# Fewer background taps ahead of attention, more folded products at the boundaries, and two lasting sets of padded key tiles in a two-layer diffusion backbone

## The chip, the cores and the metric

The kernel runs on one core of a Trainium2 chip. The metric is the device time of one execution in microseconds; lower is better. The time of the kernel before is the median of 3 runs, and a profile of one more execution is read below.

## The reference

A hybrid backbone with `D_MODEL = 1024` and two layers is computed for two groups of tokens with the same weights: a prompt of 128 tokens (its attention reads only the prompt) and a sample of 256 tokens (its attention also reads 128 cached keys). A layer has three sublayers, a feed-forward network, a mixer and a second feed-forward network, and each ends with a residual and a layer norm:

```python
h = modulate(0)
x = layer_norm(ALPHA * x + 0.5 * mod[:, 2] * swiglu(h, w_ffn_in[l, 0], w_ffn_out[l, 0]), ...)
h = modulate(1)
mix, k, v = token_mixer(h, l, p, ctx_k, ctx_v)
x = layer_norm(ALPHA * x + mod[:, 5] * mix, ...)
h = modulate(2)
x = layer_norm(ALPHA * x + 0.5 * mod[:, 8] * swiglu(h, w_ffn_in[l, 1], w_ffn_out[l, 1]), ...)
```

`token_mixer` projects its input once and cuts the result into queries, keys, values, the conv branch, the pool branch and three gates:

```python
z = h @ w_in[l] + b_in[l]                       # q, k, v, cg, pu, gt
o = rms_norm(diff_attention(q, kk, vv, lam))    # softmax of map 1 minus lam * softmax of map 2, 4 heads
att_out = o @ w_att_o[l]
u = depthwise_conv(a * sigmoid(g), conv_dw_w)   # 31 taps
conv_out = silu(layer_norm(u)) @ w_conv_o[l]
pool_out = multiscale_pool(pu) @ w_pool_o[l]
merged = ga * att_out + gc * conv_out + gp * pool_out
return merged @ w_out[l] + b_out[l], k, v
```

## The kernel before

**Tiling.** Features lie on the 128 partitions and all 384 tokens on the free axis. Each product is made from a high and a low part of weight and activation, so it is three matmuls (`mm3`, L409, L410 and L411; L732, L733 and L735 at a boundary). Weights come in 388 units of up to 128x1024; a unit is 24 matmuls of TensorE. `wh`, the high part, is a cast by ScalarE (L345), and `wl` a subtraction by VectorE (L353).

**Order.** The program is written out as one sequence, and each engine runs its part in that order. `begin(key)` (L374) opens a unit: it advances a step counter, casts the weights of the unit four ahead, runs the closures that are due at this step (`at(n, fn)` puts one n steps ahead; those due together run in the order in which they were put), then takes the low part of the weights, and then pops `bg_rate` closures from the background queue `bg` (a fraction is carried over). Only then are the unit's own matmuls written. So a matmul in a due closure stands ahead of the unit's 24, and what it waits for holds up all of them.

**The mixer** (L1057). `BG = (qk, v, pu, attention and gates, start)` gives the rate of the background queue in each stage: eight q/k units (two of them in one group), four v units (`w_v`), two pool units (`w_in` 16 and 17), then 24 gate units during which attention runs. The queue holds, in this order, 62 taps of the conv branch (one VectorE instruction each, L1118 from the third on), `conv_chain`, and 14 steps of the pool branch and its `chain`. `conv_chain` puts the stages of the conv branch's norm at `CONV_AT = (2, 4, 5, 6, 8, 9, 10, 11)` steps after it is popped: `c1` (the sum's matmuls, L1137), `c2` (broadcast of the mean, L541), `c2b`, `c3` (the squares' matmuls, L548), `c4` twice (broadcast of the scale L541, then `cz` and `cth` on ScalarE), `c5` (`ch`, L1186 on ScalarE) and `c6` (`cl`, L1192 on VectorE). The first `cp` unit, `cp0`, multiplies `ch` and `cl`; right after its `begin` a loop runs steps ahead of time until both exist.

**Attention** is ten tasks: `prompt_task` twice, then `sample_task` eight times (four heads, two blocks of queries), one task every two steps. Each has four closures at `ATT_AT` steps: `a` (scores, L1478 for the prompt, L1428 and L1429 for the sample; maxima L1483 or L1434 on VectorE; exponentials `e` on ScalarE), `b_` (L1499 or L1446 on VectorE), `c` (transposes of `e`, L1505 or L1451), `d` (product with the values L1460, whose result ScalarE reads twice, into `o`, L1463, and into `jk`, L1465). `stack(h)` makes the padded tiles of a head: `Q`, `K`, `QL` and `KL`; half of each `KL` tile is zero, written by GpSimd (L1401).

**Banks.** Six PSUM banks ("mm") serve the units and the scores. Two ("sm", from `sbank()`) serve all the rest in turn: `L1460`, `L1451`, the transposes, and the stages `c1` to `c4`. The third claim on "sm" has to wait until the first has been read.

**A boundary** (`ln_end`, L708). The norm's sum is folded into the next sublayer: the first group of four weight tiles multiplies `fold[k]`, k = 0 to 7, before mean and scale are known. `main(k0, k1)` writes 12 matmuls for each k (four tiles, three each). The order on TensorE is `main(0, 2)`, the statistics (L548, tile `tot`), `main(2, 3)`, the two broadcasts (L541), `main(3, 6)`, then the tail with k = 6 and 7. The statistics need the last tile's sums (L745 and L746 on VectorE); the broadcasts need the chain of small VectorE instructions in `ln_scale` (up to L704). There are five such boundaries with a next sublayer; i is the place in its layer of the sublayer that ends, and i = 1 is the mixer.

Of the kernel before, what the change touches and what calls it, by code (L numbers as in the profile page):

```python
# [11 lines left out]
F32 = mybir.dt.float32  # L12
F32R = mybir.dt.float32r
# [81 lines left out]

BG = (3, 3, 3, 2.5, 2)
CONV_AT = (2, 4, 5, 6, 8, 9, 10, 11)
ATT_AT = (0, 1, 2, 4)  # L100
GATE_AT = 32
# [137 lines left out]
class Kernel:  # L239
# [468 lines left out]
    def ln_end(self, b7, ab, keys):  # L708

        nc, st = self.nc, self.lns  # L710
        s = st["s"]
        l, i = divmod(s, 3)
        y7 = self.X[:, 7, :]
        sq = self.slot(name="sq")
        mm = nc.tensor.matmul
        outs = None
        if keys:
            self.fold_cols(7)
            ws = self.group(keys)
            self.held = 4  # L720
            outs = [self.bank() for _ in keys]
        for lo, hi, c in SEGS:
            nc.vector.scalar_tensor_tensor(y7[:, lo:hi], b7[:, lo:hi], st["g"][:, 0, 7, c:c + 1], y7[:, lo:hi],
                                           ALU.mult, ALU.add)
            nc.scalar.activation(sq[:, lo:hi], y7[:, lo:hi], AF.Square)

        def main(k0, k1):
            for k in range(k0, k1):
                yh, yl = self.fold[k]
                sl = slice(128 * k, 128 * k + 128)  # L730
                for (wh, wl), o in zip(ws, outs):
                    mm(o[:, :NX], wh[:, sl], yh, start=k == 0, stop=False)  # L732
                    mm(o[:, :NX], wl[:, sl], yh, start=False, stop=False)  # L733
                for (wh, wl), o in zip(ws, outs):
                    mm(o[:, :NX], wh[:, sl], yl, start=False, stop=False)  # L735

        if keys:
            ma = 2
            main(0, ma)
            self.after.append(lambda: self.fold_tile(7))  # L740
            for _ in range(8):
                self.run_after()
        merge = keys
        if merge:
            nc.vector.tensor_add(st["s1"], st["s1"], y7)  # L745
            nc.vector.tensor_add(st["s2"], st["s2"], sq)  # L746
        else:
            st["late"]()
        if keys:
            self.prep(self.cur + 1)  # L750
            if self.n_prep == self.cur + 1:
                self.prep_h()
        if merge:
            tot = self.ln_stat(st["s1"], st["s2"])
        else:
            b = self.ln_stat(y7, sq)
            tot = self.tiny(6)
            nc.vector.tensor_add(tot, st["pre"], b[:, :6])
        rm = self.ln_scale(tot)
        if keys:  # L760
            if self.half:
                self.prep_l()
            for _ in range(3):
                self.run_after()
            main(ma, 3)
        R, M = self.sbank(), self.sbank()
        self.bcast(R, rm[:, 0:3])
        self.bcast(M, rm[:, 3:6])
        if keys:
            Rs = self.slot(name="R")  # L770
            nc.scalar.copy(Rs, R[:, :NT])
            self.RM = Rs, M
            main(3, 6)

            def tail():
                for (wh, wl), o in zip(ws, outs):
                    for k in (6, 7):
                        c = 128 * k
                        self.mm3(o[:, :NX], wh[:, c:c + 128], wl[:, c:c + 128], *self.fold[k], False, k == 7)
                del ws[:]  # L780
                self.fold = [None] * 8
                self.lead = 2
        ts = [None] * 9
        xs = [None] * 8

        def mul(m):
            if m < 8:
                ts[m] = self.slot(name="t")
                nc.vector.tensor_mul(ts[m], self.X[:, m, :], R[:, :NT])

        def add(m):
            if m < 8:
                nc.vector.tensor_add(ts[m], ts[m], M[:, :NT])  # L793

        def upd(m):
            nc.scalar.activation(self.X[:, m, :], ts[m], AF.Identity, bias=self.lnbs[:, l, i, m:m + 1],
                                 scale=self.par(("lng", l, i), 1, m))

        if not keys:
            Ms = self.slot(name="M")  # L800
            nc.scalar.copy(Ms, M[:, :NT])
            mul(0)
            for m in range(8):
                mul(m + 1)
                if m % 2 == 0:
                    nc.gpsimd.tensor_add(ts[m], ts[m], Ms)
                else:
                    add(m)
            for m in range(8):
                nc.scalar.activation(self.X[:, m, :], ts[m], AF.Identity, bias=self.par(("lnb", l, i), 1, m),  # L810
                                     scale=self.par(("lng", l, i), 1, m))
                nc.sync.dma_start(self.io["y"][:, m, :], self.X[:, m, :])
            return None, None
        mul(0)
        mul(1)
        add(0)
        for m in range(8):
            fin = self.split_mod(ts[m], ab, m, m in (0, 2, 4), True)
            self.run_after()
            if m == 1:  # L820
                tail()
            if m == 2:
                self.prep(self.cur + 2)
            if m == 6 and self.n_prep == self.cur + 2:
                self.held = 0
                self.prep_h()
            add(m + 1)
            mul(m + 2)
            if m == 7 and self.half:
                self.prep_l()  # L830
            xs[m] = fin()
            self.at(2 + m // 3, lambda m=m: upd(m))
        self.held = 0
        for n, o in enumerate(outs):
            p = self.slotx(name="P")
            nc.scalar.copy(p, o[:, :NX])
            outs[n] = p
        return xs, outs
# [218 lines left out]
    def mixer(self, l, xs, outs, s):  # L1057
        nc, io = self.nc, self.io
# [29 lines left out]
        for hp in range(2):  # L1088
            for m in range(2):
                o = slice(64 - 64 * m, 128 - 64 * m)  # L1090
# [108 lines left out]
        def add_bg():  # L1199
# [3 lines left out]
            self.bg.append(conv_chain)  # L1203
        self.at(BG[4], add_bg)

# [35 lines left out]

        self.bg_rate = BG[0]
        o2 = self.kouter([("w_in", l, 0), ("w_in", l, 1)], xs, 8, KIN)
# [8 lines left out]
            self.at(1, lambda c=c, b=b: evac_qk(c, b))  # L1252


        self.bg_rate = BG[1]
        vb = [None] * 3
        for i in range(4):
            wh, wl = self.begin(("w_v", l, i))
# [121 lines left out]

        self.bg_rate = BG[2]
        for c in (16, 17):
# [5 lines left out]

        self.bg_rate = BG[3]
        oS = [self.slot(name="o") for _ in range(H)]  # L1390
# [4 lines left out]
        def stack(h):  # L1395

            Q, K = [self.slot(F32R, "Q") for _ in range(2)], [self.slot(F32R, "K") for _ in range(2)]
            QL, KL = self.slot(F32R, "QL"), [self.slot(F32R, "KL") for _ in range(2)]
            k, kks[h] = kks[h], None
            for m in range(2):  # L1400
                nc.gpsimd.memset(KL[m][64 - 64 * m:128 - 64 * m, :].bitcast(F32), 0.0)  # L1401
            for m in range(2):
                r = slice(64 * m, 64 * m + 64)
                nc.scalar.copy(Q[m][r, 0:256], qs[h][r, 128:384])
                nc.gpsimd.tensor_sub(QL[r, 0:256], qs[h][r, 128:384], Q[m][r, 0:256].bitcast(F32))
            for m in range(2):
                r = slice(64 * m, 64 * m + 64)
                nc.scalar.copy(K[m][r, :], k[r, :])
                nc.gpsimd.tensor_sub(KL[m][r, :], k[r, :], K[m][r, :].bitcast(F32))

            def move():
                for m in range(2):
                    r, o = slice(64 * m, 64 * m + 64), slice(64 - 64 * m, 128 - 64 * m)
                    nc.sync.dma_start(K[m][o, :].bitcast(F32), K[m][r, :].bitcast(F32))
                    nc.sync.dma_start(Q[m][o, 0:256].bitcast(F32), QL[r, 0:256].bitcast(F32))
            self.at(2, move)
            stk[h] = Q, K, KL
# [108 lines left out]
        for h in range(H):  # L1526
            self.at(max(n0 + sp * (2 + 2 * h) - 4, 1), lambda h=h: stack(h))
# [52 lines left out]
        for kind, mp in GP_ORDER:  # L1580
# [10 lines left out]
            for q in range(2):  # L1591
                m = 2 * mp + q
# [12 lines left out]
        for mp in range(4):  # L1605
# [3 lines left out]
            for q in range(2):  # L1609
                m = 2 * mp + q  # L1610
# [26 lines left out]
        outs = self.kouter([("w_out", l, m) for m in range(4)], mg)  # L1637
# [83 lines left out]
```

## Time and profile before

| | before |
|---|---|
| median of 3 runs | 1726.55 us (1724.62 to 1728.63) |
| the profiled execution | 1729.66 us, span 1727.8 us |
| TensorE (PE) busy | 1693.5 us, 98% of the span |
| VectorE (DVE) busy | 1325.8 us, 77% |
| ScalarE (ACT) busy | 769.6 us, 45% |
| GpSimd (POOL) busy | 342.3 us, 20% |

The page says how long each engine was busy, which waits ended last and with what clock TensorE ran (a clock of 1.00 is 2.4 GHz, 0.50 is 1.2 GHz). TensorE is busy almost throughout, so what is left to win or lose are its idle stretches and the stretches at half the clock. A busy share hides the second kind: a matmul at half the clock counts as busy for twice the time. So idle times are read from the timeline and from the list of waits, and the clock from a table of windows.

### The profile page before, as it was taken

The page shows a single profiled execution, that of the slowest core. Times are in us where ns is not written, and L with a number is a line of the kernel's source. Part 1 is how long each engine was busy: PE and PEld are TensorE (multiplying, and loading weights), DVE is VectorE, ACT ScalarE, POOL GpSimd, SP SyncE. Part 2 cuts the span into 40 slices and gives each one's busy share as a digit, 9 for nine tenths or more (in the row PEclk, how much of TensorE's full clock was granted, in tenths as well). Part 3 has the DMA queues.
Part 4 walks back from the last instruction along what each step waited for, and adds up shares of the span by engine and source line. Part 5 has one row for each costly group of instructions (what it writes and reads, how often), then busy time and mean ns, then how long its engine had stood idle before and what let it go on. Part 6 is the DMA issues. An engine that isn't in the chain of part 4 may idle for free.

```text
span 1727.8 us, 25949 instructions
## 1 busy us (share of the span) xinstructions
PE 1693.5 (98%) x9686; PEld 1666.5 (96%) x9686; DVE 1325.8 (77%) x2241; ACT 769.6 (45%) x1365; POOL 342.3 (20%) x410
## 2 busy tenths in 40 slices
PE   7999999999999999999999999999999999999997
PEld 4999999999999999999999999999899999999997
DVE  3699998799969788879777788968988788653343
ACT  3523333655554473333374333347465447333322
POOL 0000023242214510002320000325221362000022
PEclk9999999999999999999999999999999999999998
DMA  9777776435533347767636766643444342544320
GB/s 367 246 236 231 236 232 210 131 110 161 149 99 115 105 137 219 216 208 215 190 109 205 215 209 207 220 162 106 147 138 124 105 127 92 171 146 121 121 76 37
DMA packets 86638, 287.44 MB, mean 166 GB/s; under 512 B 10096, under 2 KB 17520, under 8 KB 86512
## 3 DMA queue, kind: packets, MB, share of 16 engines
q1 hardware_dynamic: 86512, 285.79, 53.2%
q8 instruction: 76, 1.25, 0.3%
q14 instruction: 50, 0.41, 0.1%
HBM read 280.51 MB, written 2.62 MB: 164 GB/s over the span
## 4 chain that ended last, share of the span: by engine, by line
PE 85%; DVE 10%; ACT 2%; issue 2%; DMA 1%; SPq 0%; ACTq 0%; POOL 0%; DVEq 0%; POOLq 0%
PE mm L409 25%; PE mm L410 25%; PE mm L411 25%; DVE wl L353 3%; DVE acc L1118 2%; DVE yl L663 1%; PE mm L434 1%; PE mm L432 1%; PE mm L431 1%; PE mm L732 1%; PE mm L735 1%; PE mm L733 1%; PE sm L541 1%; PE tot L548 1%; PE sm L1460 1%
## 5 line engine op out<-in xcount | busy, mean ns | idle before, releaser
L345 ACT CAST wh<-raw 128x1024 fp32r<-128x1024 f32 (+3 forms) x426 | 400.2, 956 | 715.4 <-issue 473.0
L409 PE MATMUL mm<-xh,wh 128*128 128x384 f32 x1796 | 609.3, 339 | 3.9 <-ACT wh L345 3.2
L410 PE MATMUL mm<-xh,wl 128*128 128x384 f32 x1796 | 607.9, 338 | 0.6 <-DVE wl L353 0.6
L411 PE MATMUL mm<-xl,wh 128*128 128x384 f32 x1796 | 605.9, 337 | 0.1
L353 DVE TENSOR_TENSOR wl<-raw,wh 128x1024 fp32r<-128x1024 f32 (+3 forms) x426 | 481.8, 1145 | 106.4 <-ACT wh L345 106.1
L409 PEld LDWEIGHTS mm<-xh,wh 128*128 128x128 f32 x1796 | 338.6, 189 | 8.5 <-ACT wh L345 4.1
L410 PEld LDWEIGHTS mm<-xh,wl 128*128 128x128 f32 x1796 | 338.3, 188 | 1.9 <-DVE wl L353 1.8
L411 PEld LDWEIGHTS mm<-xl,wh 128*128 128x128 f32 x1796 | 338.5, 188 | 0.7 <-DVE xl L855 0.7
L456 DVE SCALAR_TENSOR_TENSOR junk<-raw,scb 128x1024 bf16<-128x1024 f32 x256 | 314.2, 1227 | 4.5
L410 PE MATMUL mm<-ah,wl 128*128 128x384 f32 x704 | 237.4, 337 | 0.0
L409 PE MATMUL mm<-ah,wh 128*128 128x384 f32 x704 | 237.4, 337 | 0.0
L411 PE MATMUL mm<-al,wh 128*128 128x384 f32 x704 | 237.1, 337 | 0.0
L627 POOL TENSOR_SCALAR sq<-sq 128x384 f32<-128x384 f32 x6 | 8.7, 1446 | 789.5 <-ACT sq L624 789.5
L411 PEld LDWEIGHTS mm<-al,wh 128*128 128x128 f32 x704 | 132.2, 188 | 0.0
L410 PEld LDWEIGHTS mm<-ah,wl 128*128 128x128 f32 x704 | 132.2, 188 | 0.0
L409 PEld LDWEIGHTS mm<-ah,wh 128*128 128x128 f32 x704 | 132.2, 188 | 0.0
L876 DVE TENSOR_TENSOR al<-a,ah 128x384 fp32r<-128x384 f32 x88 | 48.6, 557 | 86.1 <-ACT ah L875 82.6
L871 DVE TENSOR_TENSOR a<-mm,si 128x384 f32<-128x384 f32 x82 | 45.5, 556 | 76.8 <-ACT si L869 71.6
L1118 DVE SCALAR_TENSOR_TENSOR acc<-U,P,acc 128x399 f32<-128x399 f32 x120 | 86.8, 773 | 0.0
L633 POOL TENSOR_TENSOR s<-s,X 128x384 f32<-128x384 f32 x30 | 42.8, 1428 | 152.9 <-DVE X L613 130.2
L663 DVE SCALAR_TENSOR_TENSOR yl<-X,ab,yh 128x128 fp32r<-128x128 f32 x80 | 66.1, 864 | 6.1 <-ACT yh L661 5.9
L855 POOL TENSOR_TENSOR xl<-hf,xh 128x384 fp32r<-128x384 f32 x40 | 44.2, 1122 | 96.6 <-DVE t L793 85.7
(286 smaller groups left out, 2062.5 us busy)
## 6 DMA issues: line engine op xcount, KB each, us to landing
raw<-in_units SPq DMA_DIRECT2D x356, 512.0 KB, 3.8
raw<-in_wmod SPq DMA_DIRECT2D x144, 512.0 KB, 4.5
raw<-in_units SPq DMA_DIRECT2D x32, 384.0 KB, 3.8
X<-in_x SPq DMA_DIRECT2D x4, 384.0 KB, 6.6
K<-K SPq DMA_DIRECT2D x16, 96.0 KB, 4.2
out_y<-X SPq DMA_DIRECT2D x8, 192.0 KB, 1.9
scb<-in_cond SPq DMA_DIRECT2D x2, 512.0 KB, 7.5
Q<-QL SPq DMA_DIRECT2D x16, 64.0 KB, 3.8
```

The source lines that it names most:

```text
L345: self.nc.scalar.copy(w[0][:, c], r[:, c])
L353: self.nc.vector.tensor_sub(wl[:, c], r[:, c], wh[:, c].bitcast(F32))
L409: mm(out, wh, xh, start=first, stop=False)
L410: mm(out, wl, xh, start=False, stop=False)
L411: mm(out, wh, xl, start=False, stop=last)
L456: self.nc.vector.scalar_tensor_tensor(self.junk, r, 1.0, self.scb[:, c, :], ALU.mult, ALU.mult, accum_out=mv[:, j, c:c + 1])
L633: nc.gpsimd.tensor_add(st["s1"], st["s1"], x)
L663: nc.vector.scalar_tensor_tensor(lo[:, a:b], x[:, a:b], self.ab[:, 0, m, c:c + 1], h[:, a:b].bitcast(F32), ALU.mult, ALU.subtract)
L855: (nc.gpsimd if pool else nc.vector).tensor_sub(xl, hf, xh.bitcast(F32))
L871: nc.vector.tensor_mul(a, u[:, :NT], sl)
L876: nc.vector.tensor_sub(lo, a, h.bitcast(F32))
L1118: nc.vector.scalar_tensor_tensor(acc[c][:, :399], U[c][:, j:j + 399], w, acc[c][:, :399], ALU.mult, ALU.add)
```

## The change

Four edits. `BG`'s rates in the v and pu stages go from 3 to 2. In `ln_end`, `main` can be limited to some of the four out tiles; after the mixer three k instead of two stand ahead of the statistics, and between the statistics and the broadcasts stands one k and, in addition, one out tile (3 matmuls) of the next. The four `KL` tiles are made once for each mixer, in two sets, and their zeros are written there, after the last q/k unit's `begin`; `stack(h)` takes set h % 2.

```diff
-BG = (3, 3, 3, 2.5, 2)
+BG = (3, 2, 2, 2.5, 2)
...
-        def main(k0, k1):
+        def main(k0, k1, a=0, z=4):
             for k in range(k0, k1):
                 yh, yl = self.fold[k]
                 sl = slice(128 * k, 128 * k + 128)
-                for (wh, wl), o in zip(ws, outs):
+                part = list(zip(ws, outs))[a:z]
+                for (wh, wl), o in part:
                     mm(o[:, :NX], wh[:, sl], yh, start=k == 0, stop=False)
                     mm(o[:, :NX], wl[:, sl], yh, start=False, stop=False)
-                for (wh, wl), o in zip(ws, outs):
+                for (wh, wl), o in part:
                     mm(o[:, :NX], wh[:, sl], yl, start=False, stop=False)
...
-            ma = 2
+            ma = 3 if i == 1 else 2
             main(0, ma)
...
-            main(ma, 3)
+            main(ma, ma + 1)
+            main(ma + 1, ma + 2, 0, 1)
         R, M = self.sbank(), self.sbank()
         self.bcast(R, rm[:, 0:3])
         self.bcast(M, rm[:, 3:6])
...
-            main(3, 6)
+            main(ma + 1, ma + 2, 1, 4)
+            main(ma + 2, 6)
...
+        KLs = [[self.slot(F32R, "KL") for _ in range(2)] for _ in range(2)]
+        for kl in KLs:
+            for m in range(2):
+                nc.gpsimd.memset(kl[m][64 - 64 * m:128 - 64 * m, :].bitcast(F32), 0.0)
...
-            QL, KL = self.slot(F32R, "QL"), [self.slot(F32R, "KL") for _ in range(2)]
+            QL, KL = self.slot(F32R, "QL"), KLs[h % 2]
             k, kks[h] = kks[h], None
-            for m in range(2):
-                nc.gpsimd.memset(KL[m][64 - 64 * m:128 - 64 * m, :].bitcast(F32), 0.0)
```

VectorE ahead of attention, layer 0, before: `wl` (L353) of the two pool units and of the first attention unit, with the taps (L1118) between, the first maxima (L1483) and the `b_` closure (L1494 to L1499).

```order
L353 TENSOR_TENSOR wl_3761<-raw_3649,wh_3760 128x1024
L1118 SCALAR_TENSOR_TENSOR acc_3250<-U_3242,P_63,acc_3250 128x399
L1118 SCALAR_TENSOR_TENSOR acc_3249<-U_3241,P_63,acc_3249 128x399
L1118 SCALAR_TENSOR_TENSOR acc_3250<-U_3242,P_63,acc_3250 128x399
L353 TENSOR_TENSOR wl_3809<-raw_3679,wh_3808 128x1024
L1118 SCALAR_TENSOR_TENSOR acc_3249<-U_3241,P_63,acc_3249 128x399
L1118 SCALAR_TENSOR_TENSOR acc_3250<-U_3242,P_63,acc_3250 128x399
L1118 SCALAR_TENSOR_TENSOR acc_3249<-U_3241,P_63,acc_3249 128x399
L1483 TENSOR_REDUCE y_3885<-mm_3879 128x2
```

And of the changed kernel, where the taps are L1121 and the maxima L1490:

```order
L353 TENSOR_TENSOR wl_3765<-raw_3657,wh_3764 128x1024
L1121 SCALAR_TENSOR_TENSOR acc_3250<-U_3242,P_63,acc_3250 128x399
L1121 SCALAR_TENSOR_TENSOR acc_3249<-U_3241,P_63,acc_3249 128x399
L353 TENSOR_TENSOR wl_3812<-raw_3686,wh_3811 128x1024
L1121 SCALAR_TENSOR_TENSOR acc_3250<-U_3242,P_63,acc_3250 128x399
L1121 SCALAR_TENSOR_TENSOR acc_3249<-U_3241,P_63,acc_3249 128x399
L1490 TENSOR_REDUCE y_3883<-mm_3877 128x2
```

One tap fewer stands behind each of the two `wl`, as behind each of the four of the v units ahead of these: six in all. They come later, in the attention stage, so that `conv_chain` is popped three steps later.

TensorE where `c1` stands, layer 0, before: the sample task's scores, its `L1460` and `L1451`, a whole unit (24 matmuls, here its first and its last), then `c1` (L1137) and the next unit.

```order
L1428 MATMUL mm_4568<-K_4311,Q_4309 128x384
L1429 MATMUL mm_4568<-KL_4314,Q_4309 128x384
L1460 MATMUL sm_4581<-vs_3212,wT_4460 128x128 x3
L1451 MATMUL sm_4588<-C_64,e_4442 128x128 x3
L409 MATMUL mm_4603<-xh_3076,wh_4305 128x384
...
L411 MATMUL mm_4603<-xl_3179,wh_4305 128x384
L1137 MATMUL sm_4635<-ones_69,as_4514 128x1 x3
L409 MATMUL mm_4656<-xh_3076,wh_4390 128x384
```

And of the changed kernel, where these lines are L1435, L1436, L1467, L1458 and L1140:

```order
L1435 MATMUL mm_4774<-K_4538,Q_4536 128x384
L1436 MATMUL mm_4774<-KL_3638,Q_4536 128x384
L1467 MATMUL sm_4787<-vs_3213,wT_4683 128x128 x3
L1458 MATMUL sm_4794<-C_64,e_4665 128x128 x3
L1140 MATMUL sm_4800<-ones_69,as_4696 128x1 x3
L409 MATMUL mm_4815<-xh_3076,wh_4532 128x384
```

The three "sm" tiles now follow each other with no unit between them. `c2` stands likewise behind the scores, `L1460` and `L1451` of the eighth and last sample task, and `c3` behind a pair `L1460`, `L1451` with no scores. Layer 1 has the same order.

ScalarE where `c5` makes `ch`, layer 0, before: the casts of weights, the evictions of gate units (`ga`, L1568) and `ch`; the last gate unit ahead of `cp0` writes `mm_5258`.

```order
L345 CAST wh_5136<-raw_4911 128x1024
L1186 ACTIVATE ch_5143<-cth_5036 128x384
L1186 ACTIVATE ch_5146<-cth_5104 128x384
L1568 ACTIVATE ga_5149<-mm_5111,bh_3195 128x384
...
L1568 ACTIVATE ga_5193<-mm_5154,bh_3195 128x384
...
L1568 ACTIVATE ga_5253<-mm_5198,bh_3195 128x384
...
L1568 ACTIVATE ga_5288<-mm_5258,bh_3195 128x384
```

And of the changed kernel, where the lines are L1189 and L1575 and the last gate unit writes `mm_5240`:

```order
L345 CAST wh_5265<-raw_5059 128x1024
L1189 ACTIVATE ch_5272<-cth_5153 128x384
L1189 ACTIVATE ch_5275<-cth_5233 128x384
L1575 ACTIVATE ga_5278<-mm_5240,bh_3195 128x384
```

The two `ch` stood three begins ahead of that of `cp0`; now they stand in it, behind its cast of weights, and `cl` follows in the same begin by way of the loop.

## Rows read from the trace of the kernel before

**Rows 1.** Page: engine, busy us, share of the span, instructions.

```profile
PE 1693.5 (98%) x9686; PEld 1666.5 (96%) x9686; DVE 1325.8 (77%) x2241; ACT 769.6 (45%) x1365; POOL 342.3 (20%) x410
```

**Rows 2.** PE's waits: who, waited for, us in total, times, longest.

```profile
PE sm L1505 <- DVE e L1499: 4.6, 2, 2.4
PE tot L548 <- DVE s L745: 3.4, 2, 1.7
```

**Rows 3.** PE timeline, mixer boundaries: start, us, line, form, count, [idle before].

```profile
589.24 0.87 PE L735 MATMUL mm<-yl,wh 128*128 128x388 f32 x4
591.81 1.24 PE L548 MATMUL tot<-ones,s 128*128 128x1 f32 x6 [1.70 <-DVE s L745]
...
606.26 0.34 PE L409 MATMUL mm<-yh,wh 128*128 128x388 f32 x1
...
1430.34 0.88 PE L735 MATMUL mm<-yl,wh 128*128 128x388 f32 x4
...
1445.77 0.34 PE L409 MATMUL mm<-yh,wh 128*128 128x388 f32 x1
```

**Rows 4.** DVE timeline at the first mixer boundary.

```profile
591.20 0.55 DVE L745 TENSOR_TENSOR s<-s,X 128x384 f32<-128x384 f32 x1
```

**Rows 5.** PE timeline at the boundary from layer 0 to layer 1's mixer.

```profile
1155.39 0.72 PE L548 MATMUL tot<-ones,s 128*128 128x1 f32 x6
...
1158.14 0.87 PE L735 MATMUL mm<-yl,wh 128*128 128x388 f32 x4
1159.21 1.60 PE L541 MATMUL sm<-C,y 128*128 128x128 f32 x12 [0.20 <-DVE y L704]
...
1167.02 0.34 PE L409 MATMUL mm<-yh,wh 128*128 128x388 f32 x1
```

**Rows 6.** Windows: length, busy us of PE, PEld, DVE, ACT, POOL, clock, DMA.

```profile
592.00:598.20 6.20, 6.20 (x24) 6.20 (x24) 4.82 (x20) 0.83 (x3) 0.00 (x0) 0.50 0.29 85
...
401.00:404.00 3.00, 3.00 (x11) 3.00 (x11) 3.00 (x6) 0.41 (x1) 0.00 (x0) 0.50 0.55 145
1243.00:1247.30 4.30, 4.30 (x17) 4.17 (x18) 4.27 (x9) 1.22 (x4) 0.00 (x0) 0.62 0.59 190
...
466.00:470.00 4.00, 3.38 (x22) 3.06 (x21) 3.85 (x10) 3.24 (x10) 0.00 (x0) 1.00 0.73 179
```

**Rows 7.** DVE and PE timelines where attention starts in layer 0.

```profile
393.35 3.24 DVE L1118 SCALAR_TENSOR_TENSOR acc<-U,P,acc 128x399 f32<-128x399 f32 x3
...
400.54 0.68 PE L1505 MATMUL sm<-C,e 128*128 128x128 f32 x2 [2.28 <-DVE e L1499]
```

**Rows 8.** All taps: shortest, median and longest in ns.

```profile
L1118 DVE SCALAR_TENSOR_TENSOR acc<-U,P,acc x120: 620/629/1387, 348.1 to 1292.0; 128x399 f32<-128x399 f32 x120
```

**Rows 9.** PE and ACT timelines in three begins of layer 0's attention.

```profile
468.13 0.37 ACT L1465 ACTIVATE jk<-sm,y 128x128 f32<-128x128 f32 x1
...
468.65 0.93 PE L541 MATMUL sm<-C,y 128*128 128x128 f32 x6 [0.62 <-ACT jk L1465]
...
475.24 0.42 PE L409 MATMUL mm<-xh,wh 128*128 128x384 f32 x1
...
476.87 0.37 ACT L1465 ACTIVATE jk<-sm,y 128x128 f32<-128x128 f32 x1
...
498.03 0.42 PE L409 MATMUL mm<-xh,wh 128*128 128x384 f32 x1
...
498.53 0.36 ACT L1465 ACTIVATE jk<-sm,y 128x128 f32<-128x128 f32 x1
```

**Rows 10.** PE, ACT and DVE timelines in the begin of `c5` and `c6`.

```profile
502.31 0.34 PE L409 MATMUL mm<-xh,wh 128*128 128x384 f32 x1
...
502.51 1.05 ACT L345 CAST wh<-raw 128x1024 fp32r<-128x1024 f32 x1 [1.53 <-PE mm L411]
503.46 0.93 ACT L1186 ACTIVATE ch<-cth 128x384 fp32r<-128x384 f32 x2
...
505.19 1.02 DVE L1192 SCALAR_TENSOR_TENSOR cl<-cth,ch 128x384 fp32r<-128x384 f32 x2
```

## The prediction

> **What bounds the kernel now.** I read the page first. PE is busy 98% of the span [rows 1], so a gain or loss can only be an idle stretch of PE or a stretch at half its clock. Next I read the list of PE's waits: the wait at attention's start, 4.6 us in two, and that of the statistics after the mixer, 3.4 us in two, are the longest that the change touches [rows 2]. Then I read the timeline around each [rows 3, 5, 7], and the windows behind them for the clock [rows 6]: behind the waits of 1.70 and 2.28 us the granted clock is 0.50, so that they cost more than their length; behind one of 2.36 us in layer 1 it is 0.62 for 4.3 us. Around a wait of 0.62 us [rows 9] it stays at 1.00 [rows 6]. Last I read the begins of attention [rows 9, 10], since by the order of the changed kernel the conv branch's stages move there.
>
> One matmul step is 0.177 us: four L735 take 0.87 us of which the last one's own 0.34 is passed through once [rows 3, 5], and (0.87 - 0.34) / 3 = 0.177.
>
> **Boundaries: a gain of 9.6 us.** Undisturbed, the stretch from the statistics to the tail's first L409 is 1167.02 - 1155.39 = 11.63 us [rows 5], of which PE waits 0.36 us for the broadcast's operand: the last L735 starts at 1158.14, four steps are over at 1158.85, L541 starts at 1159.21. That leaves 11.27 us. After the mixer of layer 0, PE is through with its products at 589.24 + 4 x 0.177 = 589.95 and reaches L409 at 606.26: 16.31 us, 5.04 too long. In layer 1 it is 1445.77 - 1431.05 = 14.72 us, 3.45 too long [rows 3]. Both hold the 1.70 us wait [rows 2, 3] and the slow clock behind it [rows 6].
>
> The change puts 12 more matmuls, 2.12 us, ahead of the statistics there, so PE arrives at 592.07; L745 ends at 591.75 [rows 4] and L548 could start at 591.81 [rows 3]. The wait goes, with 0.26 us to spare, and with it the low clock: 5.04 + 3.45 = 8.49 us. If those 0.26 us are missing, what remains is a wait of some tenths, of a length that left the clock at 1.00 [rows 6, 9]. The operands of the extra products, folded tile 2, were made many units before. At the three other boundaries with a next sublayer, 3 more matmuls (0.53 us) stand ahead of the broadcast and cover its 0.36: 1.08 us. Nothing is late behind: the same products are written, only earlier, and the broadcast starts 0.17 us later than it does now. Sum 9.57.
>
> **Attention's start: a gain of 7.7 us.** L1505 waits 2.28 us in layer 0 and 2.4 in layer 1 for VectorE's `e`, and loses about half of 3.0 us and 0.38 of 4.3 us to the clock behind it [rows 2, 6, 7]: 4.7 + 1.5 + 1.6 = 7.8, of which I keep 7.7. VectorE is the late one, and six taps fewer are queued ahead of L1499. A tap is 0.63 us in the median, 1.39 at most [rows 8], three in a row beside GpSimd's key work 3.24 us [rows 7]. At 0.55 net of the overlap of one with the next, six give 3.3 us, at 1.08 6.5; the wait needs 2.3. I take it as gone. The bound below is that VectorE, ahead of its queue, waits for the casts instead and only half of it comes through: 3.9 us. The taps themselves come later, beside gate units, where they cost VectorE what they cost it before.
>
> **Key tiles: nothing.** Eight of 16 `memset`s go from GpSimd, which is busy 20% of the span [rows 1]; the four that stay stand ahead of one k evacuation that no unit of PE multiplies before the fourth head's scores. A set is used again two heads later, four sample tasks behind the scores that read it, so its writer doesn't wait. Were GpSimd late, it would show at attention's scores, where no wait is listed now.
>
> **The conv branch's stages: a loss of 26 us.** This is the part that the diff hides. The chain is popped three steps later, and three is odd where tasks come every two steps. Before, `c1` and `c2` stood in the begins between two tasks, one unit behind the last use of the two "sm" banks, and even so `c2` waited 0.62 us for `jk` [rows 9]. Now each stands right behind `L1460` and `L1451` of the same begin, the third claim on two banks, and must wait until ScalarE has read `L1460`'s bank for `jk`. ScalarE does that behind two exponentials, which wait for VectorE's maxima.
> - `c1` and `c2`: PE is through with L1451 at 475.24, `jk` starts at 476.87 and PE could go on 0.52 us later (as 468.13 to 468.65): 477.39, a wait of 2.15 us each [rows 9].
> - `c3`, in a begin without scores: 498.53 + 0.52 - 498.03 = 1.02 us [rows 9].
> - `c4` waits for the pool's operand as before: 0.
> - `c5`, `c6` and `cp0` now share a begin. From a unit's start at 502.31, the cast comes first, then `ch`: the first of the two is there at 503.46 + 0.5 = 503.96 and the first `cl` at 505.19 + 0.5 = 505.69 [rows 10]. PE can do two matmuls at 1.7 us and goes on at about 3.5 us; against 6 steps on end that is some 3.2 us lost.
>
> Behind each of these waits stand the 24 matmuls of a unit on PE. On VectorE the scaling of `c1` (L1139) waits with it, and `wl` of the unit four ahead behind that, which PE needs three units later: nothing on the path.
>
> Per layer 2.15 + 2.15 + 1.02 + 3.2 = 8.5 us. Three of these are longer than 1.70 us, and behind waits of that length PE fell to half its clock at a price of 1.5 and 1.6 us at attention's start, about 3.1 at the first mixer boundary (6.2 us at 0.50) [rows 6]. I take 1.55, since a full unit follows here as at attention's start: 4.65 us. So 13.15 per layer, 26.3 in two. In exchange the small waits of `c1` and `c2` in layer 0 go, 0.8 us.
>
> Bounds: below, the waits are the 0.62 that was seen [rows 9], without a fall of the clock, and `cp0` costs its `ch` alone, 1.7: 3.6 per layer. Above, `jk` comes late as at 468.13, where VectorE still worked off older steps: some 2.9 us more for each of the first two, and 3.1 for each fall of the clock: 8.5 + 5.8 + 9.3 = 23.6 per layer. I take the middle since by the order VectorE has only some 7 us of work between the sixth task's maxima and the seventh's, in a span of two units and their attention work, about 10 us.
>
> The row of 0.62 us [rows 9] shows PE held by the reading of a bank claimed a unit earlier. At that size, 0.62 for each of the six waits on `jk`, and with `cp0` as above, the loss would be 3.7 + 9.5 = 13.2 us and the whole change a gain of 4.9. The Trainium skill, "Perfetto Trace Analysis", section "Matmuls", says that independent matmul groups should rotate through different PSUM banks, so that the evacuation of one overlaps the next one's matmuls. By this rule a third group behind two on two banks overlaps nothing and pays the whole evacuation, which is the sum below and speaks against the change; no row of this trace has three in a row.
>
> **Sum.** 26.3 - 9.6 - 7.7 - 0.8 = +8.2 us. Against the profiled execution's own 1729.66 us (span 1727.8 and 1.9 around it) that is 1737.9. It lies 3.1 above the median of the runs shown, so the same sum against that median is 1726.55 + 8.2 = 1734.7 us. About 0.2%, 3.45 us, is what a measurement can tell here from no change.
>
> **Rivals.**
> - *The new waits cost their length and no clock.* The threshold would lie otherwise when PE has worked at full rate until then. Then 17.0 - 18.1 = -1.1: 1725.5 us, no change. For it: none of the waits under 0.7 us lowered the clock. Against it: every wait listed from 1.70 us up did.
> - *The banks are free in time* (the other side). If PE stands behind its weights or ScalarE gets to `jk` before PE is through with `L1451`, and `ch` and `cl` are made while PE is still in the unit before, the stages cost nothing, and all gains stay: -18.1, 1708.5 us, faster. It decides where `jk` comes less than 0.5 us ahead of PE. Against it: the same `jk` stood 1.6 us behind PE in an undisturbed begin [rows 9].
> - *The upper prices*: `jk` late behind VectorE, a longer fall of the clock, or attention's wait half kept: 9 us on top, 1744 us.
> - *The change doesn't do what it says*: attention's wait stays since VectorE is held by the casts and not by taps: +7.7, 1742 us; it is in the upper case.
>
> **How the numbers follow.** Forecast 0.46, no clock 0.17, banks free 0.17, upper prices 0.20. The second case straddles the lower edge of "same", so a third of it counts as faster; a twelfth of the forecast's chance lies under 1730 us. Faster 0.17 + 0.06 = 0.23, same 0.11 + 0.04 = 0.15, slower 0.62. The range of 8 in 10 leaves out most of the banks-free case and the top of the upper one: 1714 to 1745 us; the forecast's own is 1730 to 1739.
>
> **What would show it.** In the changed kernel's trace: no wait of L548 after the mixer and clock 1.00 behind it; L1505 with a wait under 0.5 us; waits for `jk` of about 2 us at `c1` and `c2`, of 1 at `c3`, and of 3 for `ch` and `cl` at `cp0`, with a lower clock behind the long ones. If the waits for `jk` are missing, the forecast is wrong and the time is near 1708; if they are there and the clock stays at 1.00, it is near 1726.

## The result: slower, by nearly twice what was forecast

| | median | runs |
|---|---|---|
| before | 1726.84 us | 4 |
| changed | 1743.07 us | 4 |
| ratio | 1.0093, 95% interval 1.0081 to 1.0105 | |
| again on a second chip, before | 1727.34 us | 21 |
| changed | 1741.80 us | 4 |
| ratio | 1.0085, 95% interval 1.0071 to 1.0099 | |

The change costs 14.5 to 16.2 us; 8.2 were forecast. The time lies in the range of 8 in 10 (1714 to 1745 us) but outside the forecast's own (1730 to 1739); the sign is right, the size is not.

The page of the changed kernel (engine, busy us, share, instructions) shows the same work in a longer span, against [rows 1]:

```profile
PE 1696.9 (97%) x9686; PEld 1670.9 (96%) x9686; DVE 1323.2 (76%) x2241; ACT 769.7 (44%) x1365; POOL 340.1 (20%) x402
```

PE's waits in the changed kernel (who, waited for, us in total, times, longest), against [rows 2]:

```profile
PE sm L1140 <- ACT jk L1472: 7.0, 2, 3.7
...
PE sm L541 <- ACT jk L1472: 3.7, 2, 1.8
...
PE mm L409 <- ACT ch L1189: 3.1, 2, 1.6
...
PE mm L411 <- DVE cl L1195: 2.3, 2, 1.1
PE mm L409 <- DVE pm L1607: 2.0, 4, 0.5
PE sm L548 <- ACT jk L1472: 1.6, 2, 0.8
PE mm L410 <- DVE wl L353: 1.5, 3, 0.6
```

The last of these reads, in the kernel before:

```profile
PE mm L410 <- DVE wl L353: 0.6, 1, 0.6
```

Both waits that the change went for, of the statistics for L745 and of attention's start for `e`, have left the list. In their place stand `c1` (L1140), `c2` (L541), `c3` (L548) and `cp0` (`ch`, `cl`), each once in a layer, as the order had it. And behind the two boundaries that lead into a mixer PE now waits for the low part of a weight (L353: three waits instead of one), 0.48 and 0.45 us.

The timeline of PE in the changed kernel, at the first mixer boundary, at attention's start and in the begins of `c1` (both layers) and `c2`:

```profile
398.75 0.61 PE L1485 MATMUL mm<-kp,qz 128*128 128x128 f32 x4
399.19 0.38 PE L1512 MATMUL sm<-C,e 128*128 128x128 f32 x2
...
467.76 0.34 PE L1435 MATMUL mm<-K,Q 128*128 128x384 f32 x1
...
472.95 1.44 PE L1140 MATMUL sm<-ones,as 128*128 128x1 f32 x6 [3.33 <-ACT jk L1472]
...
485.01 0.34 PE L1435 MATMUL mm<-K,Q 128*128 128x384 f32 x1
...
488.71 0.38 PE L541 MATMUL sm<-C,y 128*128 128x128 f32 x1 [1.84 <-ACT jk L1472]
...
601.69 0.87 PE L736 MATMUL mm<-yl,wh 128*128 128x388 f32 x4
602.40 0.72 PE L548 MATMUL tot<-ones,s 128*128 128x1 f32 x6
...
611.47 0.34 PE L409 MATMUL mm<-yh,wh 128*128 128x388 f32 x1
...
1314.09 0.34 PE L1435 MATMUL mm<-K,Q 128*128 128x384 f32 x1
...
1319.67 0.37 PE L1140 MATMUL sm<-ones,as 128*128 128x1 f32 x1 [3.71 <-ACT jk L1472]
```

The statistics follow the products after 0.71 us with no idle time, against [rows 3], and attention's first transpose follows its neighbour at once, against [rows 7]. `c1` waits.

The windows of the changed kernel (columns as in [rows 6]): attention's start, the two mixer boundaries, then the stretches behind `c1`, `c2` and `cp0` of layer 0.

```profile
399.00:402.00 3.00, 3.00 (x21) 3.00 (x20) 2.97 (x8) 0.77 (x2) 0.00 (x0) 1.00 0.49 157
602.00:608.00 6.00, 6.00 (x45) 6.00 (x44) 5.33 (x22) 1.65 (x5) 0.00 (x0) 1.00 0.26 87
1449.00:1455.00 6.00, 6.00 (x44) 6.00 (x43) 5.26 (x22) 1.17 (x3) 0.00 (x0) 1.00 0.33 90
472.95:479.00 6.05, 6.05 (x21) 6.05 (x22) 3.47 (x9) 0.80 (x2) 0.00 (x0) 0.50 0.31 89
489.00:493.00 4.00, 4.00 (x18) 4.00 (x18) 3.27 (x8) 1.55 (x4) 0.00 (x0) 0.57 0.02 4
523.90:530.00 6.10, 4.90 (x26) 4.58 (x27) 6.10 (x22) 1.00 (x4) 0.05 (x1) 1.00 0.27 89
```

The clock is at 1.00 where it had fallen, and at half behind `c1` (6 us) and `c2` (some 3.5 us). Behind `cp0` it stays at 1.00 here. PE's busy share hides both stretches, as it hid the old ones.

### The profile page after: what moved, and what is told of

Its sections match the earlier page's. It is cut to its first block, busy times and chain, and to the rows that moved or that the text cites. A ratio compares the mean times of both kernels' runs of the same rounds, so it can differ in the third digit from the quotient of the medians.

```text
span 1740.9 us, 25947 instructions
## 1 busy us (share of the span) xinstructions
PE 1696.9 (97%) x9686; PEld 1670.9 (96%) x9686; DVE 1323.2 (76%) x2241; ACT 769.7 (44%) x1365; POOL 340.1 (20%) x402
## 3 DMA queue, kind: packets, MB, share of 16 engines
q8 instruction: 76, 1.25, 0.3%
## 4 chain that ended last, share of the span: by engine, by line
PE 90%; DVE 5%; ACT 3%; issue 1%; DMA 0%; SPq 0%; POOL 0%; ACTq 0%; DVEq 0%; POOLq 0%
PE mm L409 26%; PE mm L410 26%; PE mm L411 26%; DVE wl L353 1%; PE mm L733 1%; PE mm L734 1%; PE mm L736 1%; ACT wh L345 1%; PE mm L432 1%; PE mm L434 1%; PE mm L431 1%; PE mm L1277 1%; PE mm L1276 1%; PE mm L1275 1%; PE sm L541 1%
## 5 line engine op out<-in xcount | busy, mean ns | idle before, releaser
L353 DVE TENSOR_TENSOR wl<-raw,wh 128x1024 fp32r<-128x1024 f32 (+3 forms) x426 | 481.3, 1144 | 105.4 <-ACT wh L345 105.0
L456 DVE SCALAR_TENSOR_TENSOR junk<-raw,scb 128x1024 bf16<-128x1024 f32 x256 | 314.4, 1228 | 4.4
L1121 DVE SCALAR_TENSOR_TENSOR acc<-U,P,acc 128x399 f32<-128x399 f32 x120 | 88.8, 787 | 0.0
```

What stands on the lines that cost most here:

```text
L353: self.nc.vector.tensor_sub(wl[:, c], r[:, c], wh[:, c].bitcast(F32))
L456: self.nc.vector.scalar_tensor_tensor(self.junk, r, 1.0, self.scb[:, c, :], ALU.mult, ALU.mult, accum_out=mv[:, j, c:c + 1])
L1121: nc.vector.scalar_tensor_tensor(acc[c][:, :399], U[c][:, j:j + 399], w, acc[c][:, :399], ALU.mult, ALU.add)
```

## The experiments

**The rates alone**, on the kernel before:

```diff
-BG = (3, 3, 3, 2.5, 2)
+BG = (3, 2, 2, 2.5, 2)
```

> Only the background rates are changed; boundaries and key tiles are as before. Theory A (the loss is the conv stages standing behind the attention's two sm banks and in the begin of cp0; the boundaries gain about 10 us by themselves): the loss without the boundaries' gain, 1743 + 10 = 1753 us, with the same waits for jk of 3.3 and 3.7 us at c1, 1.8 at c2, 0.8 at c3 and of ch and cl at cp0. Rival B (the boundary or key edits are what costs): 1726 us or less, since attention's start gains.

Measured: 1753.80 us against 1725.32, ratio 1.0159 (1.0143 to 1.0175). The waits are those of the changed kernel: 3.7 us at most at `c1`, 1.9 at `c2`, 1.6 and 1.2 at `cp0`:

```profile
PE sm L1137 <- ACT jk L1465: 7.1, 2, 3.7
```

So the loss is in this line. The wait of attention's start (L1505) has left this list too, so its gain comes from the same line. (One of its four runs took 1747.75 us, the others 1753.48 to 1754.64; why they part is not settled.)

**Everything but the rates**: the changed kernel with `BG = (3, 3, 3, 2.5, 2)`.

> The changed kernel with the background rates of before: boundaries and key tiles alone. Theory A: the gain of the boundaries alone, about 10 us: 1717 us, no wait of L548 after the mixer, the clock 1.00 behind it, attention's first wait of 2.3 us still there and no new wait for jk. Rival B: 1740 us or more. Rival C (the profiled execution of before had longer stretches at the low clock than its other runs, so that the gain is overstated): 1720 us.

Measured: 1717.42 us against 1725.32, ratio 0.9960 (0.9946 to 0.9974), as Theory A had it. No wait of L548 is left, and `c1` to `cp0` have no new one. Attention's first wait, which was to stay at 2.3 us, is 1.6 us at most; the clock behind it stays at 1.00.

**The same rates, the conv stages between the tasks**: the changed kernel with

```diff
-CONV_AT = (2, 4, 5, 6, 8, 9, 10, 11)
+CONV_AT = (1, 3, 4, 5, 7, 8, 9, 10)
```

> The changed kernel with each entry of CONV_AT one step smaller, so that the conv stages stand two steps later than before instead of three, between the attention tasks and not in their begins, and ch a begin ahead of cp0. Theory A: nearly all of the loss of the conv stages goes (28 us in the two traces), small waits of up to 1 us a layer stay: 1716 us, waits for jk under 0.7 us and clock 1.00. Rival D (VectorE is late from the taps that were moved into attention, wherever the stages stand): at least 1735 us, with waits of PE for VectorE or for jk of 2 us and more.

Measured: 1714.18 us against 1725.32, ratio 0.9939 (0.9926 to 0.9951). The taps still come late, and VectorE still has them beside attention, but of the long waits for `jk`, `ch` and `cl` this is what its list of PE's waits still has, and `pm` once a layer as before:

```profile
PE sm L1140 <- ACT jk L1472: 1.1, 1, 1.1
PE sm L409 <- ACT jk L1472: 1.1, 2, 0.6
PE mm L409 <- DVE pm L1607: 1.0, 2, 0.5
```

One step of the table is worth 26 to 27 us (11.1 faster than before instead of 14.5 to 16.2 slower). The longest wait is above the 0.7 us of Theory A, and behind it the clock fell, which was not expected either (window below, in the last section). Rival D is out: no wait of 2 us is left, so it is where the stages stand that costs, with the same taps for VectorE.

**The same place, other banks**: the changed kernel, in `c1`, `c2` and `c3`

```diff
-                b = self.sbank()
+                b = self.bank()
```

> The changed kernel with c1, c2 and c3 in banks of the six-bank ring instead of the two sm banks; their place in the order is unchanged. Theory A: the waits at c1, c2 and c3 go with their stretches at the low clock (11.6 and 12.0 us by the trace), those at cp0 stay (1.6 for ch, 1.1 for cl, clock 1.00): 1743 - 23.6 = 1719.5 us. Rival D: the matmuls of c1 to c3 wait for VectorE's own operands or the units behind them wait for wl, so 1735 us or more.

Measured: 1721.54 us against 1725.32, ratio 0.9979 (0.9970 to 0.9988). The order is untouched, and `c1` to `c3` no longer wait; `cp0` does, in its list of PE's waits:

```profile
PE mm L409 <- ACT ch L1189: 3.1, 2, 1.6
...
PE mm L411 <- DVE cl L1195: 2.3, 2, 1.1
```

That is 18 to 20 us below the changed kernel; Theory A had 23.6. So the third claim on two banks is the cause at `c1` to `c3`, and the shared begin that at `cp0`. Against the kernel with the smaller `CONV_AT`, `cp0` and what follows it cost 7.4 us, 3.7 in a layer. In this trace the clock fell behind `cp0` in layer 1 and not in layer 0 (windows in the last section).

**The kernel before, profiled again.**

> The kernel before, unchanged, profiled once more: how far its rows are those of one execution. Theory A: the first profile (1729.66 us) was a slow draw, 4 us above the median of 15 runs on another chip, because the stretches at half the clock behind the five long waits differ from execution to execution; here some of them are shorter or missing at waits of the same length, and the span is 1721 to 1725 us. Rival: the rows repeat within 0.5 us each and the 4 us lie in the stream of the weights.

Measured: 1727.74 us, ratio 1.0001 (0.9992 to 1.0010), span 1725.9 us. The waits repeat, the clock behind them does not. Its waits and windows, attention's start in both layers:

```profile
PE sm L1505 <- DVE e L1499: 4.6, 2, 2.4
...
PE tot L548 <- DVE s L745: 3.3, 2, 1.7
```

```profile
400.30:403.30 3.00, 3.00 (x17) 2.88 (x18) 3.00 (x6) 0.83 (x1) 0.00 (x0) 1.00 0.46 139
1241.00:1244.00 3.00, 3.00 (x17) 2.88 (x18) 3.00 (x6) 0.88 (x1) 0.00 (x0) 1.00 0.54 162
```

The same idle time of 2.3 and 2.4 us as in [rows 2, 7], and 17 matmuls at full clock where [rows 6] has 11 at half. The 1.5 and 1.6 us of low clock there belong to the execution that was read, not to the wait. The span lies just above the 1721 to 1725 us of Theory A. Behind the mixer's boundaries the clock fell here too.

**The changed kernel again, beside it.**

> The changed kernel again, on the same chip and in the same rounds as the other kernels. Theory A: the waits for jk, ch and cl repeat within 0.2 us, the stretches at half the clock behind c1 and c2 repeat less well; the time is 17 us above the kernel before's. Rival: 14 us or less, the first comparison having been of runs that don't belong together.

Measured: 1741.80 us against 1727.34, the second ratio above; 14.5 us, between the two expectations. Its waits are those of the first profile within 0.2 us.

**The key tiles alone**, on the kernel before.

```diff
+        KLs = [[self.slot(F32R, "KL") for _ in range(2)] for _ in range(2)]
...
-            QL, KL = self.slot(F32R, "QL"), [self.slot(F32R, "KL") for _ in range(2)]
+            QL, KL = self.slot(F32R, "QL"), KLs[h % 2]
...
```

> The kernel before with the two lasting sets of key tiles alone. The prediction said no difference: 0 us. Theory E (read from the trace of the kernel with the old background rates, where attention's first wait fell from 2.3 to 1.6 us and the clock behind it stayed at 1.00): 4 to 5 us faster, since GpSimd's zeros no longer stand between its subtractions for the first head, VectorE's taps beside them are done sooner, and the shorter wait no longer lowers the clock.

Measured: 1727.90 us against 1727.34, ratio 1.0006 (0.9997 to 1.0015): no difference, as predicted. Theory E falls. Attention's first waits are 4.7 us in two; behind that of layer 0 the clock stayed at 1.00, behind that of layer 1 it fell, with nothing changed at either. Why the same tiles beside the changed boundaries go with a first wait of 1.6 us (above) is not shown; no difference in time is seen there either.

**The boundaries alone**, on the kernel before: `ma = 3 if i == 1 else 2` and the further products ahead of the broadcasts.

> The kernel before with the products at the boundaries alone. The prediction said 9.6 us faster, so 1716 us where the kernel before has 1725.3. Theory E: 1725.3 - (8 - 4.5) = some 4 to 6 us faster only, since boundaries and key tiles together gave 7.9; rival: 8 us faster, and the key tiles give nothing.

Measured: 1718.99 us against 1727.34, ratio 0.9951 (0.9937 to 0.9965): 8.35 us faster, as the rival had it. The changed kernel differs from this one, in the same rounds, by 22.8 us, which is the rates' net cost, the key tiles being nothing.

**VectorE freed ahead of `c1`**: the changed kernel with the modulation steps (L456) behind the eighth sample task.

```diff
-        self.mod_rate = 0.4
         for m in range(8):
-            if m == 7:
-                self.mod_rate = 0
             gate(26 + m, tcp, (0, m))
...
             if kind == "w_in":
+                self.mod_rate = 0.56 if mp > 2 else 0
                 gate(34 + mp, tcp, (1, mp))
                 continue
+            self.mod_rate = 0
             w = self.begin(("cp", l, mp))
```

> The changed kernel with VectorE's three modulation steps of the mixer (L456, two instructions of 1.2 us each) written behind the eighth sample task instead of between the gate units ahead of it; nothing else moves. Theory F (c1's wait was 3.3 and 3.7 us by the waits view and not 2.1 because VectorE was still behind and took the seventh task's maxima 2.0 to 2.4 us after the scores began): the maxima come 0.6 us after the scores, c1's wait is 2.0 us, and with the shorter stretch at half the clock behind it the time falls by 4 to 7 us, to 1735 to 1738. Rival G (the exponentials and ScalarE's own queue set the wait): c1 still waits 3.3 us or more and the time stays at 1742.

Measured: 1740.41 us against 1727.60, ratio 1.0077 (1.0065 to 1.0090). First VectorE and ScalarE ahead of `c1` in the changed kernel, from the sixth task's scores on, then the same with PE in this one:

```profile
457.68 0.34 PE L1435 MATMUL mm<-K,Q 128*128 128x384 f32 x1
...
461.73 1.02 DVE L1441 TENSOR_REDUCE y<-mm 128x1 f32<-128x384 f32 x2
...
469.80 1.02 DVE L1441 TENSOR_REDUCE y<-mm 128x1 f32<-128x384 f32 x2
...
471.06 0.58 ACT L1444 ACTIVATE e<-mm,y 128x384 f32<-128x384 f32 x1 [2.00 <-DVE y L1442]
...
472.43 0.37 ACT L1472 ACTIVATE jk<-sm,y 128x128 f32<-128x128 f32 x1
```

```profile
468.40 1.02 DVE L1441 TENSOR_REDUCE y<-mm 128x1 f32<-128x384 f32 x2 [0.31 <-PE mm L1436]
...
469.66 0.58 ACT L1444 ACTIVATE e<-mm,y 128x384 f32<-128x384 f32 x1 [0.52 <-DVE y L1442]
...
471.04 0.37 ACT L1472 ACTIVATE jk<-sm,y 128x128 f32<-128x128 f32 x1
471.56 0.83 PE L1140 MATMUL sm<-ones,as 128*128 128x1 f32 x6 [1.85 <-ACT jk L1472]
```

In the changed kernel VectorE takes the seventh task's maxima 2.04 us after the scores began (467.76), with no idle time ahead of them: it was late. Here it waits for PE. `c1` starts 471.56 - 467.85 = 3.71 us after the scores instead of 5.19, and the seventh to the eighth task's scores take 2.8 and 3.1 us less in the two layers. Theory F holds for the wait and fails for the time, which was to fall by 4 to 7 us: the medians of two chips differ by 1.4 us, which their intervals do not part. By the starts of the same instructions in the two traces, 0.6 and 2.0 us come back between the eighth task and `cp0`, where VectorE now has these steps and `cp0` waits 2.1 us for `ch`, and 1.7 and 1.5 between `cp0` and the first product of attention's output. There the clock fell behind `cp0` in both layers, as it had not in the changed kernel; in layer 0:

```profile
523.84:526.84 3.00, 3.00 (x9) 3.00 (x10) 3.00 (x15) 0.00 (x0) 0.00 (x0) 0.50 0.61 183
```

A wait was moved, not removed.

**Both cures**: the smaller `CONV_AT` and the six-bank ring.

> The changed kernel with both cures: each CONV_AT one step smaller, and c1, c2 and c3 in banks of the six-bank ring. Theory A: as the kernel with the smaller CONV_AT alone, less its one wait of 1.1 us for jk at c1: 11 to 13 us faster than before, 1713 us. Rival: the claims on the six-bank ring hold up scores or units, and it is 2 us or more slower than the kernel with the smaller CONV_AT alone.

Measured: 1711.99 us against 1727.60, ratio 0.9914 (0.9901 to 0.9928): 15.6 us faster than before. The wait for `jk` at `c1` is gone (1.0 us for VectorE's sum is in its place). It is more than the 11 to 13 us of Theory A, and it beats both kernels.

## Why the prediction was right in its mechanism and wrong in its size

| term | predicted | by the traces before, after | by the traces of boundaries alone, after again |
|---|---|---|---|
| boundaries | -9.6 | -10.0 | -8.35 (timed, alone) |
| attention's start, two layers | -7.7 | -8.5 | -5.35 |
| conv stages, two layers, net of old waits | +25.5 | +28.3 | +28.7 |
| sum | +8.2 | +9.9 (unrounded) | +15.0 |

The terms of the traces are differences between the starts of the same instructions (milestones): from the first scores of the prompt to the first of the sample for attention's start (22.97 and 23.08 us before, 18.80 and 18.79 after, 21.43 and 21.52 with the boundaries alone), and from the fifth sample task to the first `w_out` product for the conv stages (+13.4 and +14.9; +13.5 and +15.2). The last column adds up to about the 14.5 us that were timed, but it takes its first term from the timing. By traces alone the sums fall short: the spans of the first pair differ by 13.1 us where the terms give 9.9, and those of the second profiles of before and after by 14.2 where they give 11.8 (-11.5, -5.4, +28.7). The rest, 3.2 and 2.4 us, lies outside the three stretches; about 1.0 of it are the new waits for L353.

Of the 6.8 us between the forecast and the last sum, 3.2 are the conv stages, 2.35 attention's start and 1.25 the boundaries.

- **Boundaries: right.** The arrival at 592.07 us was to be 0.26 us behind L548's earliest start, and no wait is left. The gain of 9.6 lies in the interval around 8.35. "Nothing is late behind" was wrong in a small way: in the two mixers PE reaches a weight's low part (L353) before VectorE has made it, and the stretch from the boundary to attention is 0.5 us longer in both layers, with the boundaries alone too. That takes back what the broadcast gained at two of the three other boundaries.
- **Key tiles: right**, 0.6 us within an interval that holds zero.
- **Attention's start: right, mis-sized.** The wait is gone with six taps fewer. The term "1.5 + 1.6" for the low clock was priced as sure; the second profile of before has the waits without it. Against the second pair that overstates the gain by 2.35 us; the first pair, which has these falls, gives 8.5.
- **The conv stages: right in place and cause, mis-sized at `c1`.** The banks alone take the loss at `c1` to `c3` away, the steps alone all of it but one wait of 1.1 us. The step that failed is "I take the middle since by the order VectorE has only some 7 us of work between the sixth task's maxima and the seventh's, in a span of two units and their attention work, about 10 us". Work and span were of that size in layer 0 (469.80 - 461.73 = 8.07 us and 467.76 - 457.68 = 10.08), but VectorE came to the sixth task 4.05 us after its scores, out of the taps and two modulation steps ahead of it, so that 4.05 + 8.07 - 10.08 = 2.04 us were left at the seventh. In layer 1 a modulation step stands between the two. The wait was 472.95 - (467.76 + 1.62) = 3.57 us, and 3.96 in layer 1, instead of 2.15; with VectorE in time it is 471.56 - (467.85 + 1.62) = 2.09, the predicted value. The clock behind it fell for 6 us, a price of 3.0 instead of 1.55. So `c1` cost 6.6 us in layer 0 and about 7.0 in layer 1 where 3.7 were forecast, 6.2 us too little in all; it was luck that `cp0` gave half of that back.
- `c2` came as told (488.71 - 485.01 - 1.62 = 2.08 us, price of the clock 4.0 x 0.43 = 1.7), `c3` too (0.8 us by the list of waits and 0.2 of start-up), and `cp0` lost 3.0 of the predicted 3.2 us. Its fall of the clock, 1.55 us, did not come in either layer of the two profiles. Its idle time is in two pieces of 1.56 and 1.14 us, but that is not the reason: behind the same two pieces the clock did fall in layer 1 of the rates alone and of the other banks.
- Not foreseen: the `cp` units wait for `pm` twice a layer instead of once, 0.5 us by the list of waits, some 0.65 with the start-up.

In layer 0 that is 3.6 + 3.0 + 2.1 + 1.7 + 1.0 + 3.0 + 0.65 = 15.05 us. Less the old waits of `c1` and `c2` that is 13.7, against +13.4 of the milestones. The old waits are 1.3 us by the traces and not the 0.8 of the prediction: before, the fifth to the seventh task's scores take 22.9 us in layer 0 and 21.6 in layer 1, where `c1` and `c2` do not wait. Of the rivals, the banks that are free in time are out, by the waits. "No clock" was right for `cp0` and wrong for `c1` and `c2`. The upper price held at `c1` alone. That its 1744 us lie beside the measured 1743.07 is in part luck: attention's wait, one of its three conditions, did not stay at all.

What stays open: why the rates alone cost 28.5 us in one set of rounds and 22.8 in the difference of two kernels in another. One part is seen: in the trace of the rates alone the clock fell behind `cp0` in layer 1 too, and the stretch of the conv stages there is 1.4 us longer than in the changed kernel.

## What to carry to other kernels

A background rate is also a clock: six background steps fewer moved a chain by an odd number of steps against tasks of period two, and its short matmuls landed behind two others in a ring of two banks. When work is moved along a schedule, look at what its dependants now stand beside, and at the ring of buffers that they share, before counting what the move itself saves. Where a wait is priced, ask which other engine must be in time for the price to hold, and price a fall of the clock as something that may or may not come; a second profile of the same kernel shows which falls are its own.

## What the runs showed of the hardware that was not expected

The clock's fall does not follow from the length of one wait. Behind attention's first wait (2.25 to 2.39 us) it fell in three of eight instances: both of the first profile of before, one of two with the key tiles alone, none of two in the second profile of before, none of two with the boundaries alone:

```profile
401.40:404.40 3.00, 3.00 (x17) 2.88 (x18) 3.00 (x6) 0.82 (x1) 0.00 (x0) 1.00 0.43 146
1238.20:1241.20 3.00, 3.00 (x18) 2.88 (x19) 3.00 (x6) 0.80 (x1) 0.00 (x0) 1.00 0.43 147
```

These two windows are of the boundaries alone, behind waits of 2.25 and 2.36 us. Behind the shorter wait of the statistics after the mixer (1.63 to 1.70 us) it fell in all eight instances of the four profiles that have it, and behind `c1` and `c2` right behind two groups on the same banks (1.84 to 3.74 us) in all sixteen of four profiles. Behind `cp0` with its two waits of 1.56 and 1.14 us it fell in two of eight instances: of the run with other banks, layer 0 and layer 1 read:

```profile
512.95:515.95 3.00, 3.00 (x17) 3.00 (x18) 3.00 (x15) 0.00 (x0) 0.00 (x0) 1.00 0.59 180
1348.15:1351.15 3.00, 3.00 (x9) 3.00 (x10) 3.00 (x15) 0.00 (x0) 0.00 (x0) 0.50 0.61 175
```

And behind the wait of 1.15 us at `c1` in the run with the smaller `CONV_AT` it fell as well:

```profile
466.40:469.40 3.00, 3.00 (x11) 3.00 (x11) 2.41 (x6) 1.08 (x2) 0.00 (x0) 0.51 0.43 138
```

In the second profile of before, the stretch behind the mixer's boundary in layer 0 reads:

```profile
590.79:597.62 6.83, 6.83 (x27) 6.83 (x28) 4.18 (x19) 0.41 (x2) 0.00 (x0) 0.50 0.36 97
592.00:594.00 2.00, 2.00 (x7) 2.00 (x8) 1.72 (x13) 0.00 (x0) 0.00 (x0) 0.50 0.72 221
594.00:596.00 2.00, 2.00 (x8) 2.00 (x7) 1.72 (x6) 0.00 (x0) 0.00 (x0) 0.50 0.10 41
596.00:598.00 2.00, 2.00 (x14) 2.00 (x12) 0.08 (x1) 0.48 (x1) 0.00 (x0) 0.59 0.59 131
598.00:600.00 2.00, 2.00 (x14) 2.00 (x13) 2.00 (x5) 0.50 (x2) 0.00 (x0) 1.00 0.32 131
```

The half clock lasts 6.8 us there (first line) and ends while the matmuls run on; 7 or 8 matmuls start in 2 us where 14 do at full clock.
